# One run per partition for a scan's operand stacks, and modulation moved from the scan to a projection

## The chip, the core and the metric

The kernel runs on one core of a Trainium2 chip. The core has five engines that work beside each other and meet at semaphores: PE (matrix products), DVE (vector), ACT (scalar functions and copies), POOL (a second vector engine) and SP, which here issues almost all transfers on one queue. Sixteen DMA engines carry the packets of all queues, the packets with the engines' own instructions among them. The metric is the device time of one execution in microseconds (us); lower is better.

## The reference

Two layers act on one residual stream of 1024 latent and 256 context tokens with 1024 channels, in float32. Layer 0 mixes over time with a two-directional RWKV-7 recurrence, layer 1 with attention; each is followed by an MLP. Cut to what matters here:

```
def modulate(h, shift, scale): return h * (1 + scale) + shift

def _wkv_step(state, inp):
    r, w, k, v, kk, bvec = inp
    sa = einsum('bhvk,bhk->bhv', state, -kk)
    state = state * w[:, :, None, :] + sa[..., None] * bvec[:, :, None, :] + v[..., None] * k[:, :, None, :]
    y = einsum('bhvk,bhk->bhv', state, r)
    return state, y

for i in range(DEPTH):
    m_l = split(silu(c) @ w_mod[i] + b_mod[i], 6)         # shift, scale and gate, twice
    m_c = split(silu(c_ctx) @ w_mod[i] + b_mod[i], 6)
    h = modulate(rms_norm(x, norm_mix[i]), m[0], m[1])
    x = x + m[2] * mix(h)                                 # r, k, v projections, 2 scans, readout, wo
    x = x + m[5] * mlp(modulate(rms_norm(x, norm_mlp[i]), m[3], m[4]))
```

The scan runs over the context first, and its end states start the scans over the latent tokens.

## The kernel before

The work runs in stages: norm and first modulation parts (to about 100 us); the k projection with three small low-rank products and the modulation of layer 1 (to 345 us); the r and v projections with the preparation of the scan beside them (345 to 1025 us); the scan itself (1025 to 1523 us); readout and output projection (to 1707 us); MLP, attention, MLP.

A modulation part (`mod_part`) makes 512 of a layer's 6144 values. It loads eight tiles `wmod` of 128x512 (256 KB each), multiplies them with the activated `c` in four quarters of PE (`ps_mod`, L191), has ACT copy the sums to `mrow` (L195), and turns them with four small products (L198). Layer 0 has twelve parts. Its first four are made at the start; numbers 4 to 11 are needed only after the scan, and `mod_some` and `kick` spread them over the scan.

The scan is worked in chunks of 32 tokens: 40 steps, each for four pairs of channel tiles (`Chain.step`, pairs staggered by `staggered`). One step of one pair is four groups of eight products on PE: `ps_x` (L848) from the state `SV` and the stack, `ps_x` again (L854) with the chunk's inverse `T`, `ps_s` (L868), which gives the next state, and `ps_y` (L877), the output. Between them ACT and DVE copy results and POOL spreads the inverse (L830).

The operands of the scan lie in DRAM scratch. The tensor `d_ST` holds the stacks: for each of 128 partitions, four pairs, nine units (eight with the tiles `AR` and `G`, the ninth with the inverses `TTo`), 40 chunks, 64 values. Preparation writes it (L676 for `AR` and `G`, L720 for `TTo`). Two chunks are a granule, and every two steps `Lanes.load` fetches the next granule's parts for two of the four pairs at a time (`lp` 0 or 1): the stacks `ST` (L805), the lane states `LS` (L808, from `d_LS`), and the values `SV` (L811, from `d_V`).

Preparation (`Prep`) takes 80 half units through PE, ACT, DVE and POOL, and `weave` hands them out beside the projections. After each group of 32 chunks, `Prep.invert` inverts 32x32 triangles in 31 dependent rounds on POOL and DVE (`To` and `Tn`, L712 and L713), between two transposes on DVE (`Tm`, L699, and `TTo`, L717). There are five such inversions; the last is that of the fourth pair over the latent chunks, which the scan's first four granules, those of the context, don't need.

Each engine runs its instructions in the order in which they were written, moved by a scheduler that simulates the times when the program is built. What it thinks comes first stands first in an engine's queue and holds up what stands behind it.

Of the kernel before, what the change touches and what calls it, by code (L numbers as in the profile page):

```python
# [14 lines left out]
PSUM = bass.MemoryType.PSUM  # L15
# [3 lines left out]
KT = 8  # L19
# [7 lines left out]
NC = PB // 32  # L27
# [353 lines left out]
def rwkv_consts(k):  # L381
    k.ctile("PT", [128, KT, 2, 41], pool=k.rc)
    k.ctile("zr", [128, KT, NT // 128, 2], pool=k.rc)
    dt = lambda n, shape: k.dram.tile(shape, F32, name="d_" + n, tag="d_" + n)
    S = k.S
    S["lg1"] = dt("lg1", [128, NT])
    S["h"] = [dt(f"h{ct}", [128, NT]) for ct in range(KT)]
    S["in"] = [dt(f"in{ct}", [128, 3, NT]) for ct in range(KT)]
    S["vn"] = [dt(f"vn{ct}", [NT, 128]) for ct in range(KT)]
    S["V"] = dt("V", [2, 2, 32, 20, 2, 4, 64])  # L390
    S["LS"] = dt("LS", [2, 20, 2, 32, 4, 2, 2, 2, 64])
    S["ST"] = dt("ST", [128, 4, 9, 40, 64])


def own_rows(st, pr, u, n, half, anti):


    return st[half * 64:half * 64 + 64, pr, (half ^ anti) * 4 + u, n:n + NC].rearrange("p c e -> p (c e)")


def head_sums(k):
# [33 lines left out]
def phase_a(k, hs, ps, ls, pg):  # L435
# [3 lines left out]
    tc, nc, S = k.tc, k.nc, k.S  # L439
    hp = hs.enter_context(tc.tile_pool(name="hp", reuse_waits="tile", bufs=1, side="right"))  # L440
    h = [hp.tile([128, NT], F32, name=f"h{ct}", tag=f"h{ct}") for ct in range(KT)]
    pt = ps.enter_context(tc.tile_pool(name="pt", reuse_waits="tile", bufs=1, space=PSUM))
    with ExitStack() as e2:
        xp = e2.enter_context(tc.tile_pool(name="xp", reuse_waits="tile", bufs=1))
        wp = e2.enter_context(tc.tile_pool(name="wmp", reuse_waits="tile", bufs=8))
# [127 lines left out]
class Prep:  # L573
# [23 lines left out]
    def half(self, U, ct, blk, u0, d, B):  # L597

        k, nc, S, wk = self.k, self.k.nc, self.k.S, self.wk
        t0, n0 = blk * PB, first_chunk(d, blk)  # L600
# [72 lines left out]
        yield  # L673
        for t, anti in ((AR, 0), (G, 1)):
            for half in range(2):
                nc.sync.dma_start(out=own_rows(S["ST"], pr, ct2 * 2 + d, n0, half, anti), in_=t[half * 64:half * 64 + 64].rearrange("p c e -> p (c e)"))  # L676
        for h in range(2):
            for f in range(2):
                p = slice(h * 64 + f * 32, h * 64 + f * 32 + 32)
# [12 lines left out]
    def invert(self, Lr, dst, engs):  # L692


        k, nc, ip = self.k, self.k.nc, self.ip
        M = ip.tile([128, 2, 32, 32], F32, name="Tm", tag="Tm")
        N = [ip.tile([128, 32, 32], F32, name="Tn", tag=f"Tn{d}") for d in range(2)]
        for d in range(2):
            nc.vector.transpose(M[:, d], Lr[d].rearrange("p u j -> p j u"))  # L699
            yield  # L700
            nc.gpsimd.memset(N[d], 0.0)
            nc.gpsimd.memset(N[d].rearrange("p a b -> p (a b)")[:, 0:1024:33], 1.0)
            yield
        for i in range(31):
            for d in range(2):
                e = getattr(nc, engs[d])
                s = i if d == 0 else 31 - i
                rows, cols = (slice(s + 1, 32), slice(0, s + 1)) if d == 0 else (slice(0, s), slice(s, 32))
                r, w = rows.stop - rows.start, cols.stop - cols.start
                t = ip.tile([128, 256], F32, name="To", tag=f"To{d}")  # L710
                o = t[:, :r * w].rearrange("p (a b) -> p a b", b=w)
                e.tensor_tensor(o, M[:, d, rows, s:s + 1].to_broadcast([128, r, w]), N[d][:, s:s + 1, cols].to_broadcast([128, r, w]), ALU.mult)  # L712
                e.tensor_tensor(N[d][:, rows, cols], N[d][:, rows, cols], o, ALU.add)  # L713
                yield
        out = ip.tile([128, 32, 2, 32], F32, name="TTo", tag="Tm")
        for d in range(2):
            nc.vector.transpose(out[:, :, d].rearrange("p u j -> p j u"), N[d])  # L717
            yield
        for pr, u0, nch, n0 in dst:
            nc.sync.dma_start(out=k.S["ST"][:, pr, 8, n0:n0 + nch], in_=out[:, u0:u0 + nch].rearrange("p u d j -> p u (d j)"))  # L720
        yield

    def units(self, kinds, eng):
# [51 lines left out]
class Lanes:  # L775
# [24 lines left out]
    def load(self, k, lp, i):  # L800

        nc, S = k.nc, k.S
        ST, LS, SV = self.gp.tile([128, 2, 9, 2, 64], F32, name="ST", tag=f"ST{lp}"), self.LS[lp][i % 2], self.SV[i % 2]
        self.ST[lp, i] = ST
        nc.sync.dma_start(out=ST.rearrange("p l u c e -> p (l u) (c e)"), in_=S["ST"][:, lp * 2:lp * 2 + 2, :, 2 * i:2 * i + 2].rearrange("p l u c e -> p (l u) (c e)"))  # L805
        for h in range(2):
            anti = slice(64 - h * 64, 128 - h * 64)
            nc.sync.dma_start(out=LS[anti, h].rearrange("p l d a e c -> p (l d a e c)"), in_=S["LS"][h, i, :, :, lp * 2:lp * 2 + 2].rearrange("b s l d a f e -> (b s) (l d a f e)"))  # L808
# [197 lines left out]
def phase_ab(k, xstack):  # L1006
# [3 lines left out]
    with ExitStack() as es:  # L1010
# [13 lines left out]
        wk = ws.enter_context(tc.tile_pool(name="wk", reuse_waits="tile", bufs=1, side="right"))  # L1024
        prep, eng = Prep(k, wk, ip, pw, pg), iter(['gpsimd', 'gpsimd', 'gpsimd', 'vector', 'gpsimd', 'vector', 'gpsimd', 'vector', 'gpsimd', 'vector'])
        drain(itertools.islice(rproj, 13))
        weave(_chain([rproj, vproj]), 6 * KT - 13 + 4 + 6 * KT - LEAD, (PREP_PIECES, prep.units((0, 1, 2, None, 3), eng)))
        drain(prep.inv)
        for st in (ps, ls, ws):
            st.close()  # L1030
        mods = iter(range(5, 12))

        def mod_some(n):
            for _ in range(n):
                yield from mod_part(k, 0, next(mods), wm, pw, "pw", L)
# [15 lines left out]

        with ExitStack() as cs:
            L = Lanes(k, cs)
            wm = cs.enter_context(tc.tile_pool(name="wm", reuse_waits="tile", bufs=4))
            with tc.issue_after(k.late.ins):
                for lp in range(2):
                    L.load(k, lp, 0)
            kick = mod_part(k, 0, 4, wm, pw, "pw", L, groups=1)
            drain(itertools.islice(kick, 4))
            middle = _chain([_chain([r.center(b, False), r.scale(b, False)]) for b in (1, 2) for r in ro])  # L1060
            weave(staggered([Chain(k, L, p, y[p]).run() for p in range(4)]), 16 * Chain.n + 16, (1, kick, 12, 13), (8, kick, 16, 40), (13 * 7, mod_some(7), 16),
                  (4 * 4 + 4 * 7, early(), 16 * 5, 16 * 31), (8 * 7, middle, 16 * 33))
# [426 lines left out]
```

## Time and profile before

| | us |
|---|---|
| median of three runs | 4116.77 |
| lowest and highest run | 4102.94, 4118.79 |
| profiled execution | 4115.24 |
| its span in the trace | 4113.5 |

The profiled execution is 1.7 us longer than its span, and 1.5 us below the median. In the page, PE is busy for 3673.9 us of the span, DVE for 2179.5, POOL for 1576.1, ACT for 1523.1. PE's busy share is lowest in the preparation and in the scan, where the transfers' share is high as well; from 1605 us on PE is hardly ever idle and the transfers take a tenth to a quarter of their engines. What the change touches lies between 345 and 1523 us.

### The profile page before, as it was taken

To read this page: it belongs to the slowest core of one execution; us is meant where nothing else is said; L and a number is where in the kernel's file an instruction comes from. 1 tells how busy PE (TensorE), PEld (TensorE's weight loads), DVE (VectorE), ACT (ScalarE), POOL (GpSimd) and SP (SyncE) were. 2 spreads that over 40 slices of the span, in tenths; PEclk is the share of its full clock that TensorE was granted. 3 is DMA by queue.
4 is the path that set the end of the run, shared out by engine and by line. 5 is a ranking of instruction groups with operands and counts; after the bars stand their busy time and mean duration, and the time that the engine had idled before them with its cause. 6 is when DMAs were issued, how large, how long until landed. Compare 5 with 4: busy or idle time off the path is not lost.

```text
span 4113.5 us, 70717 instructions
## 1 busy us (share of the span) xinstructions
PE 3673.9 (89%) x28100; PEld 2803.7 (68%) x28100; DVE 2179.5 (53%) x3707; ACT 1523.1 (37%) x3222; POOL 1576.1 (38%) x1451
## 2 busy tenths in 40 slices
PE   7999866784677779999999999899999999999998
PEld 3656655673455657888888888775444477888886
DVE  6327789987653477533333333657676443333324
ACT  5656555554344443421222222433444422221122
POOL 3105686663532253521111111534787633222221
PEclk9999865885787789999999999999999999999999
DMA  8455776676888864111111111232110111111112
GB/s 286 130 161 158 176 189 160 159 185 153 211 207 202 201 164 118 60 42 36 37 36 39 39 39 44 77 101 87 32 31 16 56 42 47 46 44 49 47 53 70
DMA packets 398714, 414.77 MB, mean 101 GB/s; under 512 B 152992, under 2 KB 282272, under 8 KB 397744
## 3 DMA queue, kind: packets, MB, share of 16 engines
q1 hardware_dynamic: 397424, 408.94, 36.9%
q8 instruction: 221, 3.62, 0.4%
q0 software_dynamic: 960, 1.31, 0.2%
q14 instruction: 109, 0.89, 0.1%
HBM read 294.99 MB, written 117.11 MB: 100 GB/s over the span
## 4 chain that ended last, share of the span: by engine, by line
PE 70%; DVE 12%; issue 5%; DMA 5%; POOL 4%; ACT 2%; SPq 2%; DVEq 0%; POOLq 0%; ACTq 0%
PE ps_pj L275 47%; PE ps_av L1355 4%; PE ps_s L868 3%; PE ps_m L1232 2%; PE ps_mod L191 2%; PE ps_s L1395 2%; PE ps_s L1396 2%; POOL n_t L377 2%; PE ps_y L877 1%; PE ps_lo L419 1%; PE ps_x L848 1%; PE ps_x L854 1%; DVE To L712 1%; DVE Tn L713 1%; DMA LS<-d_LS 1%
## 5 line engine op out<-in xcount | busy, mean ns | idle before, releaser
L259 POOL TENSOR_TENSOR w_lo<-w_raw,w_hi 128x512 fp32r<-128x512 f32 (+1 forms) x292 | 475.9, 1631 | 1597.4 <-ACT w_hi L257 1549.8
L275 PE MATMUL ps_pj<-xh,w_hi 128*128 128x512 f32 (+1 forms) x1712 | 626.6, 367 | 4.2 <-ACT w_hi L257 3.8
L275 PE MATMUL ps_pj<-xh,w_lo 128*128 128x512 f32 (+1 forms) x1712 | 618.4, 365 | 8.1 <-POOL w_lo L259 8.0
L275 PE MATMUL ps_pj<-xl,w_hi 128*128 128x512 f32 (+1 forms) x1712 | 623.7, 365 | 0.6 <-DVE xl L998 0.6
L1115 DVE SCALAR_TENSOR_TENSOR xr<-ps_pj,c_mod,xr 128x512 f32<-128x512 f32 (+1 forms) x368 | 251.9, 686 | 566.6 <-PE ps_pj L275 559.8
L257 ACT CAST w_hi<-w_raw 128x512 fp32r<-128x512 f32 (+1 forms) x292 | 216.7, 742 | 836.4 <-PE ps_pj L275 645.2
L275 PE MATMUL ps_pj<-hid_l,w_hi 128*128 128x512 f32 (+1 forms) x1280 | 474.4, 371 | 0.0
L275 PE MATMUL ps_pj<-hid_h,w_hi 128*128 128x512 f32 (+1 forms) x1280 | 473.2, 371 | 0.0
L275 PE MATMUL ps_pj<-hid_h,w_lo 128*128 128x512 f32 (+1 forms) x1280 | 469.8, 370 | 0.0
L1139 DVE TENSOR_TENSOR m_q<-m_r 128x512 f32<-128x512 f32 x160 | 187.8, 1174 | 407.5 <-ACT m_r L1137 406.8
L275 PEld LDWEIGHTS ps_pj<-xh,w_lo 128*128 128x128 f32 x1712 | 323.2, 190 | 61.6 <-POOL w_lo L259 10.4
L275 PEld LDWEIGHTS ps_pj<-xh,w_hi 128*128 128x128 f32 x1712 | 325.0, 190 | 59.0 <-ACT w_hi L257 5.8
L275 PEld LDWEIGHTS ps_pj<-xl,w_hi 128*128 128x128 f32 x1712 | 324.8, 190 | 52.9 <-issue 1.4
L1406 POOL TENSOR_TENSOR acc<-acc,p 128x1024 f32<-128x1024 f32 x122 | 295.4, 2421 | 58.9 <-ACT p L1399 54.5
L275 PEld LDWEIGHTS ps_pj<-hid_h,w_hi 128*128 128x128 f32 x1280 | 241.4, 189 | 44.2
L275 PEld LDWEIGHTS ps_pj<-hid_h,w_lo 128*128 128x128 f32 x1280 | 241.1, 188 | 43.8
L275 PEld LDWEIGHTS ps_pj<-hid_l,w_hi 128*128 128x128 f32 x1280 | 241.4, 189 | 43.2
L275 PE MATMUL ps_pj<-xhi,w_hi 128*128 128x512 f32 (+1 forms) x576 | 229.4, 408 | 25.1 <-ACT xhi L479 19.6
L1399 ACT ACTIVATE p<-ps_s 128x1024 f32<-128x1024 f32 x160 | 163.8, 1024 | 230.6 <-PE ps_s L1396 229.5
L275 PE MATMUL ps_pj<-xlo,w_hi 128*128 128x512 f32 (+1 forms) x576 | 224.0, 390 | 8.8 <-DVE xlo L480 8.8
L1236 DVE TENSOR_REDUCE mc<-ps_m 128x1 f32<-128x512 f32 x256 | 174.7, 690 | 99.9 <-PE ps_m L1232 96.2
L830 POOL TENSOR_TENSOR T<-ST,c_qmask 128x256 f32<-128x256 f32 x160 | 118.9, 744 | 280.4 <-PE ps_x L854 197.0
(238 smaller groups left out, 7071.2 us busy)
## 6 DMA issues: line engine op xcount, KB each, us to landing
wmod<-in_wmod SPq DMA_DIRECT2D x192, 256.0 KB
ST<-d_ST SPq DMA_DIRECT2D x40, 1152.0 KB
w_raw<-in_m SPq DMA_DIRECT2D x64, 512.0 KB
w_raw<-in_m SPq DMA_DIRECT2D x128, 256.0 KB
d_ST<-AR SPq DMA_DIRECT2D x160, 128.0 KB
d_LS<-KT SPq DMA_DIRECT2D x320, 64.0 KB
d_ST<-G SPq DMA_DIRECT2D x160, 128.0 KB
LS<-d_LS SPq DMA_DIRECT2D x80, 256.0 KB
```

Source lines behind the costliest of these rows:

```text
L191: i = nc.tensor.matmul(ps[q:q + 32, :W], k.c["sc"][:, kt, :], w, start=(kt < groups), stop=(kt >= KT - groups), tile_position=(0, q))
L257: nc.scalar.copy(hi, raw)
L259: getattr(nc, eng).tensor_tensor(lo, raw, hi.bitcast(F32), ALU.subtract)
L275: i = nc.tensor.matmul(ps[:, :n], w[:, sl], x[:, t0:t0 + n], start=a, stop=z)
L830: k.nc.gpsimd.tensor_tensor(self.T, t.to_broadcast([128, 2, 4, 32]), k.c["qmask"].unsqueeze(1).to_broadcast([128, 2, 4, 32]), ALU.mult)
L868: nc.tensor.matmul(pst[h * 64:h * 64 + 64, ct2, d, :], ls[:, h, ln, d, ct2, :, c], sv(h, ct2, d), start=True, stop=True, tile_position=(0, ...
L1115: k.nc.vector.scalar_tensor_tensor(x[:, t0:t0 + n], ps[:, :n], g, x[:, t0:t0 + n], ALU.mult, ALU.add)
L1139: nc.vector.tensor_tensor(q[:, :n], r[:, :n], r[:, :n], ALU.mult)
L1236: line(nc.vector.tensor_reduce(mc[:, t + u, t0 // 512:t0 // 512 + 1], ps, AX.X, ALU.max), "v")
L1355: line(nc.tensor.matmul(st["av"][e * 64:e * 64 + 64], k.V[:, kt, ct // 2 * 64:ct // 2 * 64 + 64], p[:, e], start=(kt == 0), stop=(kt == 9) ...
L1399: nc.scalar.activation(p, ps, AF.Exp)
L1406: (nc.vector if ct == KT - 1 and kt % 3 == 2 else nc.gpsimd).tensor_tensor(st["acc"], st["acc"], p, ALU.add)
```

## The change

The stacks' tensor is laid out anew: `d_ST` is now ordered by partition, pair of pairs, granule, pair, unit, chunk, so that all that one load of `ST` takes lies in one piece per partition. A load that read 18 runs of 512 bytes per partition reads one of 9216 bytes. The stores pay for it: one of `AR` or `G` wrote one run of 2048 bytes per partition and now writes four of 512; one of `TTo` wrote one run of 8192 (or 2048) bytes and now writes 16 (or 4) of 512.

The modulation parts 4 to 11 of layer 0 leave the scan. `r_and_mods` hands them out beside the 35 pieces of the r projection that are left when the preparation begins, two pieces of modulation or so to one of the projection. They take their sums in the PSUM pool `pt`. The first of them, which alone was made in one piece of PE instead of four (`groups=1`), is now made like the others.

```
-    S["ST"] = dt("ST", [128, 4, 9, 40, 64])
+    S["ST"] = dt("ST", [128, 2, 20, 2, 9, 2, 64])
...
+def granules(st, pr, u, n, num, rows=slice(None)):
+    return st[rows, pr // 2, n // 2:(n + num) // 2, pr % 2, u].rearrange("p i c e -> p i (c e)")
...
-        nc.sync.dma_start(out=ST.rearrange("p l u c e -> p (l u) (c e)"), in_=S["ST"][:, lp * 2:lp * 2 + 2, :, 2 * i:2 * i + 2]...)
+        nc.sync.dma_start(out=ST.rearrange("p l u c e -> p (l u c e)"), in_=S["ST"][:, lp, i].rearrange("p l u c e -> p (l u c e)"))
...
+        rest = 6 * KT - 13
+        def r_and_mods():
+            with tc.tile_pool(name="wm", reuse_waits="tile", bufs=4) as wm:
+                weave_in = _chain([mod_part(k, 0, c, wm, k.pt, "pt") for c in range(4, 12)])
+                for n, _ in enumerate(rproj):
+                    drain(itertools.islice(weave_in, 8 * 9 * (n + 1) // rest - 8 * 9 * n // rest))
+                    yield
+                drain(weave_in)
-        weave(_chain([rproj, vproj]), 6 * KT - 13 + 4 + 6 * KT - LEAD, (PREP_PIECES, prep.units(...)))
+        weave(_chain([r_and_mods(), vproj]), rest + 4 + 6 * KT - LEAD, (PREP_PIECES, prep.units(...)))
...
-            weave(staggered([...]), 16 * Chain.n + 16, (1, kick, 12, 13), (8, kick, 16, 40), (13 * 7, mod_some(7), 16), (..., early(), ...), (..., middle, ...))
+            weave(staggered([...]), 16 * Chain.n + 16, (..., early(), ...), (..., middle, ...))
```

What this does to the queues shows at three places. The first is PE in the scan, somewhat before its middle: before, products of the modulation stand between the pairs' groups.

```order
L868 MATMUL ps_s<-SV_10461,LS_10465 64x64 x8
L877 MATMUL ps_y<-SV_10461,ST 32x64 x8
L198 MATMUL ps_mod<-c_msel,mrow 128x2
L848 MATMUL ps_x<-SV_10460,ST 32x64 x8
L854 MATMUL ps_x<-X,T 32x64 x8
L868 MATMUL ps_s<-SV_10461,LS_10465 64x64 x8
L877 MATMUL ps_y<-SV_10461,ST 32x64 x8
```

All of these `ps_mod` rows are gone from the scan. The second place is PE about the middle of what is left of the r projection, where they stand now, between projection (`ps_pj`, with the split inputs `xhi`, `xlo`) and preparation (`ps_g`, and `ps_l`, the low-rank products):

```order
L275 MATMUL ps_pj<-xlo,w_hi 128x256
L198 MATMUL ps_mod<-c_msel,mrow 128x2
L666 MATMUL ps_g<-AR,KB 64x64 x16
L198 MATMUL ps_mod<-c_msel,mrow 128x2 x3
L275 MATMUL ps_pj<-xhi,w_lo 128x256
L275 MATMUL ps_pj<-xhi,w_hi 128x256
L275 MATMUL ps_pj<-xlo,w_hi 128x256
L275 MATMUL ps_pj<-xhi,w_lo 128x256
L275 MATMUL ps_pj<-xhi,w_hi 128x256
L693 MATMUL ps_z<-c_rkb,kd 128x2 x2
```

Preparation's products stand behind them in PE's queue. The third place is SP's queue at the scan's start. Before, the store of the last inverses (`d_ST<-TTo`, 2048 values) comes after the loads of the first granules; these are the rows that end with it, the second and third granules' loads and modulation weights ahead of it:

```order
L808 DMA LS_10465<-d_LS 64x1024 x2
L811 DMA SV_10461<-d_V 32x512 x8
L186 DMA wmod<-in_wmod 128x512 x8
L808 DMA LS_10462<-d_LS 64x1024
L805 DMA ST<-d_ST 128x18x128
L808 DMA LS_10462<-d_LS 64x1024
L808 DMA LS_10464<-d_LS 64x1024
L805 DMA ST<-d_ST 128x18x128
L808 DMA LS_10464<-d_LS 64x1024
L811 DMA SV_10460<-d_V 32x512 x8
L186 DMA wmod<-in_wmod 128x512 x4
L720 DMA d_ST<-TTo 128x2048
```

Now it stands ahead of the first load of `LS` and `SV`:

```order
L560 DMA d_vn_133<-vt_sb 128x4x128
L810 DMA ST<-d_ST 128x2304 x4
L560 DMA d_vn_133<-vt_sb 128x4x128
L566 DMA d_V<-d_vn_133 32x32x64 x2
L725 DMA d_ST<-TTo 128x16x128
L813 DMA LS_10730<-d_LS 64x1024 x2
L813 DMA LS_10732<-d_LS 64x1024 x2
L816 DMA SV_10728<-d_V 32x512 x8
L813 DMA LS_10731<-d_LS 64x1024 x2
```

The four loads of `ST` (two granules, both halves) go ahead, but `LS` and `SV` of the first granule now wait in SP's queue for the last inversion. On DVE, likewise, the clearing of `SV` (L790 and L792 before) now stands behind the last inversion, where it stood between `Tm` and the rounds.

More of the change, by code (lines that the diff above doesn't have):

```diff
@@ L391, in rwkv_consts @@
     S["LS"] = dt("LS", [2, 20, 2, 32, 4, 2, 2, 2, 64])
-    S["ST"] = dt("ST", [128, 4, 9, 40, 64])
+    S["ST"] = dt("ST", [128, 2, 20, 2, 9, 2, 64])
 def own_rows(st, pr, u, n, half, anti):
-    return st[half * 64:half * 64 + 64, pr, (half ^ anti) * 4 + u, n:n + NC].rearrange("p c e -> p (c e)")
+    return granules(st, pr, (half ^ anti) * 4 + u, n, NC, slice(half * 64, half * 64 + 64))
+def granules(st, pr, u, n, num, rows=slice(None)):
+    return st[rows, pr // 2, n // 2:(n + num) // 2, pr % 2, u].rearrange("p i c e -> p i (c e)")
 def head_sums(k):
@@ L441, in phase_a @@
     h = [hp.tile([128, NT], F32, name=f"h{ct}", tag=f"h{ct}") for ct in range(KT)]
-    pt = ps.enter_context(tc.tile_pool(name="pt", reuse_waits="tile", bufs=1, space=PSUM))
+    pt = k.pt = ps.enter_context(tc.tile_pool(name="pt", reuse_waits="tile", bufs=1, space=PSUM))
     with ExitStack() as e2:
@@ L675, in half @@
             for half in range(2):
-                nc.sync.dma_start(out=own_rows(S["ST"], pr, ct2 * 2 + d, n0, half, anti), in_=t[half * 64:half * 64 + 64].rearrange("p c e -> p (c e)"))
+                nc.sync.dma_start(out=own_rows(S["ST"], pr, ct2 * 2 + d, n0, half, anti), in_=t[half * 64:half * 64 + 64].rearrange("p (i c) e -> p i (c e)", c=2))
         for h in range(2):
@@ L719, in invert @@
         for pr, u0, nch, n0 in dst:
-            nc.sync.dma_start(out=k.S["ST"][:, pr, 8, n0:n0 + nch], in_=out[:, u0:u0 + nch].rearrange("p u d j -> p u (d j)"))
+            nc.sync.dma_start(out=granules(k.S["ST"], pr, 8, n0, nch), in_=out[:, u0:u0 + nch].rearrange("p (i c) d j -> p i (c d j)", c=2))
         yield
@@ L804, in load @@
         self.ST[lp, i] = ST
-        nc.sync.dma_start(out=ST.rearrange("p l u c e -> p (l u) (c e)"), in_=S["ST"][:, lp * 2:lp * 2 + 2, :, 2 * i:2 * i + 2].rearrange("p l u c e -> p (l u) (c e)"))
+        nc.sync.dma_start(out=ST.rearrange("p l u c e -> p (l u c e)"), in_=S["ST"][:, lp, i].rearrange("p l u c e -> p (l u c e)"))
         for h in range(2):
@@ L1026, in phase_ab @@
         drain(itertools.islice(rproj, 13))
-        weave(_chain([rproj, vproj]), 6 * KT - 13 + 4 + 6 * KT - LEAD, (PREP_PIECES, prep.units((0, 1, 2, None, 3), eng)))
+        rest = 6 * KT - 13
[6 more added lines that the diff above has]
+                drain(weave_in)
+        weave(_chain([r_and_mods(), vproj]), rest + 4 + 6 * KT - LEAD, (PREP_PIECES, prep.units((0, 1, 2, None, 3), eng)))
         drain(prep.inv)
@@ L1030, in phase_ab @@
             st.close()
[L1031 to L1035, printed above, removed]
         rn = es.enter_context(tc.tile_pool(name="rn", reuse_waits="tile", bufs=1))
@@ L1053, in phase_ab @@
             L = Lanes(k, cs)
-            wm = cs.enter_context(tc.tile_pool(name="wm", reuse_waits="tile", bufs=4))
             with tc.issue_after(k.late.ins):
@@ L1057, in phase_ab @@
                     L.load(k, lp, 0)
-            kick = mod_part(k, 0, 4, wm, pw, "pw", L, groups=1)
-            drain(itertools.islice(kick, 4))
             middle = _chain([_chain([r.center(b, False), r.scale(b, False)]) for b in (1, 2) for r in ro])
-            weave(staggered([Chain(k, L, p, y[p]).run() for p in range(4)]), 16 * Chain.n + 16, (1, kick, 12, 13), (8, kick, 16, 40), (13 * 7, mod_some(7), 16),
-                  (4 * 4 + 4 * 7, early(), 16 * 5, 16 * 31), (8 * 7, middle, 16 * 33))
+            weave(staggered([Chain(k, L, p, y[p]).run() for p in range(4)]), 16 * Chain.n + 16, (4 * 4 + 4 * 7, early(), 16 * 5, 16 * 31), (8 * 7, middle, 16 * 33))
         ips.close()
```

## The prediction

> **What bounds the kernel now.** I read the chain of waits first, then windows by stage, then the scan alone.
>
> ```profile
> span 4113.5 us, 70717 instructions
> PE 70%; DVE 12%; issue 5%; DMA 5%; POOL 4%; ACT 2%; SPq 2%; DVEq 0%; POOLq 0%; ACTq 0%
> ```
>
> PE ends most steps. "Issue" is time in which PE waits for nothing that the profile shows, about 200 us. The windows, whose columns are us, busy time of PE, PEld, DVE, ACT and POOL with counts, granted clock, DMA share and GB/s:
>
> ```profile
> 345.00:450.00 105.00, 99.20 (x798) 81.96 (x797) 79.39 (x137) 65.78 (x160) 48.68 (x64) 0.97 0.72 187
> 450.00:550.00 100.00, 77.46 (x736) 65.90 (x737) 80.69 (x130) 56.06 (x148) 79.00 (x122) 0.87 0.73 173
> 650.00:750.00 100.00, 70.57 (x519) 55.18 (x517) 98.49 (x196) 58.52 (x148) 50.28 (x74) 0.61 0.72 168
> 1300.00:1400.00 100.00, 72.02 (x2137) 57.95 (x2129) 37.40 (x99) 42.96 (x168) 24.08 (x33) 0.79 0.87 204
> ```
>
> At the head of the r projection PE is full; later in the preparation DVE is. In the scan no engine is full, and the transfers fill 0.87 of their engines. The chain of waits of the scan alone (1100 to 1523 us), and its transfers:
>
> ```profile
> by line: PE ps_s L868 24.4%; issue 23.4%; PE ps_y L877 13.3%; PE ps_x L848 10.0%; PE ps_x L854 9.2%; PE ps_mod L191 4.3%; DMA LS<-d_LS 3.2%; DVE SV L872 2.5%; PE ps_mod L198 2.0%; ACT SV L861 1.2%; DMA ro_v<-d_V 0.9%; DMA SV<-d_V 0.8%; DVE
> q1 hardware_dynamic: 99435, 81.55, 81.2%
> q8 instruction: 74, 1.21, 1.3%
> ST<-d_ST SPq DMA_DIRECT2D x34, 1152.0 KB
> ```
>
> PE's products are the bound, and 23.4% of 423 us, 99 us, is "issue". Queue q8 explains it: 74 packets with 1.21 MB, 16 KB each, are PE's own instructions, one packet per 423 / 74 = 5.72 us. In the timeline the gaps lie 128 matmuls (128 weight loads beside them) apart: 256 instructions of 64 bytes are such a packet. So I cut the scan there; each window is one packet's work and the gap behind it (four in a row, which are one granule, and the scan's last, without transfers):
>
> ```profile
> 1393.04:1399.99 6.95, 3.58 (x127) 3.00 (x127) 2.44 (x7) 2.59 (x10) 1.47 (x2) 1.00 1.13 263
> 1399.99:1406.59 6.60, 5.45 (x128) 4.60 (x127) 2.52 (x8) 2.59 (x10) 1.46 (x2) 0.54 1.10 243
> 1406.59:1411.22 4.63, 4.63 (x125) 4.11 (x128) 1.21 (x4) 2.48 (x10) 1.46 (x2) 0.54 0.30 87
> 1411.22:1414.98 3.76, 3.12 (x141) 2.65 (x133) 3.04 (x8) 2.70 (x11) 1.46 (x2) 1.00 0.39 107
> 1517.64:1521.88 4.24, 3.77 (x137) 3.02 (x132) 3.84 (x11) 3.42 (x14) 0.00 (x0) 1.00 0.02 4
> ```
>
> The same 128 matmuls, give or take those in flight at a cut, take 3.8 to 4.6 us where transfers leave room, and 6.6 to 7.0 us where a load of `ST` fills the engines (share over 1.0): PE then idles for its next packet, which waits behind the load. [...]
>
> **The change part by part.**
>
> *Modulation out of the scan.* In the scan's chain L191 and L198 hold 4.3 + 2.0% of 423 us, 26.6 us: −27.
>
> *Modulation into the r projection.* PE gets those 27 us. About half falls into the first 105 us, which have no room for it (99.20 busy), half behind them, where there is room: +13. On SP and the DMA engines, 64 loads of 256 KB come to 16.8 MB (here and below, 1 MB is 10^6 bytes). The price of long rows:
>
> ```profile
> 4.00:20.00 16.00, 0.13 (x1) 0.16 (x2) 9.97 (x21) 11.05 (x23) 0.00 (x0) 1.00 0.98 375
> 1605.00:1707.00 102.00, 101.56 (x882) 93.39 (x882) 47.39 (x87) 34.89 (x71) 35.35 (x28) 0.98 0.25 76
> 1307.00:1311.00 4.00, 2.42 (x93) 2.03 (x92) 2.28 (x6) 2.04 (x9) 1.47 (x2) 1.00 1.04 235
> ```
>
> At 375 / 0.98 = 383 GB/s (input tiles) they take 44 us of full engines, at 76 / 0.25 = 304 (weights) 55. Spread over some 250 us this lifts the share from 0.72 to about 0.93: near the limit, not over it. Four buffers make SP wait for PE and PE for SP; behind a late weight stand preparation's stores on SP and its products on PE. I take +5 for that (0 to +40). ACT's eight copies fit into its idle time (65.78 of 105 busy). The mixing for v stands later, behind the last modulation weights in SP's queue; DVE's work is the same, so I add nothing.
>
> *Stores in 512-byte runs.* 320 stores of 128 KB (41.9 MB) go from 20,480 packets to 81,920, and those of `TTo` (5.2 MB) from 1024 to 10,240. No row isolates such a store. If they move like the 512-byte loads (235 / 1.04 = 226 GB/s, the last row) instead of 383, they take 185 instead of 109 us, +76 of engine time over 650 us, share +0.12. But the r stretch moves 187 GB/s at 0.72, that is 260 at full share, with most packets still shorter (43792 of 70009 under 512 bytes), so the lower end is zero. DVE covers either, unless the share reaches 1.0. I take 0 (0 to +20).
>
> ```profile
> DMA packets 70009, 52.99 MB, mean 180 GB/s; under 512 B 43792, under 2 KB 55696, under 8 KB 69850
> ```
>
> *Loads in 9216-byte runs.* One load is 1.18 MB: at 226 GB/s 5.2 us, at 383 3.1, at 304 3.9. I take 3.1, as those tiles too go to all 128 partitions in long rows. So 2.1 us less for each of 40 loads, 84 us of engine time. What of it reaches PE is the wait of one packet of instructions per load: of four windows per granule, two are caught by a load. I let these fall from 6.8 to 5.0 us, by most of the load's 2.1, as a packet may still meet `LS` or `SV`; the other two stay at 4.2, the mean of the three light rows. Mean 4.6. The scan has 40 steps of four pairs, four groups of 2560 records:
>
> ```profile
> L848 PE MATMUL ps_x<-SV,ST x2560: 216/219/316, 1044.1 to 1519.0; 128*32 128x64 f32 x197
> ```
>
> 10,240 matmuls are 80 windows: 80 x 4.6 = 368 us. At 5.72 they would be 458; the 90 us between are the 27 of modulation, about 13 of the 17 us that 3.2 + 0.8% of the chain are waits for `LS` and `SV`, and 50 of the 99 us of "issue". Ends: caught windows not shortened, 5.36 on average (5.72 less modulation's 26.6 / 74; 429 us); none caught, with the clock up, 3.8 as in the fourth row (304).
>
> *The scan's start.* It now waits for the last inversion. Before, that lay beside the first steps:
>
> ```profile
> 1016.45 1.11 PE L553 MATMUL ps_vt<-c_ident,pj_sb 128*128 128x128 f32 x4 [8.45 <-ACT vt_sb L554]
> 1044.08 3.18 PE L848 MATMUL ps_x<-SV,ST 128*32 128x64 f32 x48 [26.51 <-DMA SV<-d_V]
> 1021.51 3.73 DVE L699 STREAM_TRANSPOSE Tm<-Lr 128x1024 f32<-128x1024 f32 x2 [6.83 <-DMA d_ST<-TTo]
> 1025.15 0.61 SPq L805 DMA_DIRECT2D ST<-d_ST  x1
> 1099.85 0.37 SPq L720 DMA_DIRECT2D d_ST<-TTo  x1
> 1021.00:1093.00 72.00, 15.76 (x31) 16.24 (x31) 0.69 0.88 209
> 1021.00:1093.00 72.00, 15.36 (x31) 17.77 (x31) 0.69 0.88 209
> ```
>
> From `Tm` to the store it took 78 us, but the rounds alone (the last two rows, L712 and L713, with DVE's and POOL's busy time) need 16.24 + 17.77 = 34 us on POOL. In the new order only four spreadings of `T` come between. With transposes and gaps I put it at 47. `Tm` itself waited 6.83 us for its buffer; that store now goes out much earlier, so it starts at 1014.7 plus the 18 us of the r stretch: 1033. The store follows at 1080; behind it twelve loads are issued at about 0.55 us each (the rows below) and the last lands, 9 us, which covers the clearing of `SV` on DVE (six at 0.91): first `ps_x` at 1089. At the end, 3 us for the staggered pairs.
>
> ```profile
> 1291.97 1.09 SPq L808 DMA_DIRECT2D LS<-d_LS  x2
> 1026.67 0.91 DVE L790 MEMSET SV<- 32x1024 f32 x1 [0.25 <-issue]
> ```
>
> *Sum.* 1089 + 368 + 3 = 1460 for the end of the scan, 1523 before: −63. By terms: 18 for preparation, 27 more for the start (45 against 1044), 21 back because the old scan's first steps crept (its 479 us from 1044 to 1523 are 21 over 458), −90 for the pace, 3 for the end. From 4115.24 this gives 4052 us, and 2 more against the median, 4116.77. Nothing after 1523 us changes.
>
> **The rivals.** (1) *Slower: the inversion holds the scan.* If the r stretch saturates its queues, everything up to `Tm` slips, and SP's order leaves no cover. At 4.6 per window the gain is gone when the first `ps_x` comes at 1152, 63 us later than I put it; with a slip of 90, 4142 us. For it: the share near 0.93, SP in order, PE 0.94 busy at the head. Against it: PE has 20 to 30 us free in each later 100.
>
> (2) *The layout does nothing for PE.* Either a load's engine time stays at 5.2 us or a packet of instructions waits as long behind fewer, larger runs. Then the windows stay at 5.36, the scan takes 429 us and ends at 1521: 4113 us. [...] The same holds if the 9216-byte runs are cut up again.
>
> (3) *The gaps go altogether.* If light loads rarely meet a packet, windows average 3.8 and the clock, 0.54 behind a gap in the third row, stays up: 304 us, an end at 1396, 3988.
>
> **How the numbers follow.** Mine 0.54 (4015 to 4088: ten to fifteen us of start or 0.3 us of a window either way), rival three 0.16, rival two 0.15, rival one 0.15, of which two thirds cost over 0.5%. 0.5% (21 us) is about what a measurement can tell from no change. Faster: 0.54 + 0.16 + a little of rival one less the end of mine, 0.70; same 0.19; slower 0.11. The range of eight in ten reaches from near rival three to just over rival two: 3992 to 4116.
>
> **What would show it.** Right: the packets of q8 in the scan come 4.6 us apart, the chain's "issue" there halves, `ST` no longer fills the engines for 5 us, no `ps_mod` lies in the scan, and the first `ps_x` stands behind `TTo`. Wrong: windows still over 7 us beside `ST` (rival two); `Tm` after 1070 us (rival one); or 512-byte stores that lift the share of the preparation to 1.0.

## The result, and the profile after

The changed kernel is slower: 4140.91 us median of five runs (4134.76 to 4149.1) beside 4106.83 for the kernel before (five runs, 4102.94 to 4118.79). The ratio is 1.0076, its 95% interval 1.0052 to 1.0099. I had forecast 4052 us, 0.984. The profiled execution after took 4134.76 us with a span of 4133.0, 19.5 us more than before. It was the shortest of its five, and the profiled one before (4115.24) lay above its median, so the two profiles lie closer together than the medians. Every kernel below has one profiled execution; the times of one kernel differ by up to 21 us from execution to execution, so a difference of ten us between two scans is no more than a hint unless it comes again in other pairs.

The scan first. These rows of the view by tile give the count, the durations (ns) and the start of the first and the last product `ps_x`; the last `ps_y` ends some 4 to 5 us behind it. The first row is the kernel after; the others are two experiments told below, the layout alone (L853) and the moved modulation alone (L848). The kernel before has 1044.1 to 1519.0, as quoted in the prediction.

```profile
L853 PE MATMUL ps_x<-SV,ST x2560: 216/219/317, 1103.4 to 1535.6; 128*32 128x64 f32 x197
```
```profile
L853 PE MATMUL ps_x<-SV,ST x2560: 216/219/316, 1051.8 to 1518.4; 128*32 128x64 f32 x197
```
```profile
L848 PE MATMUL ps_x<-SV,ST x2560: 216/219/317, 1094.5 to 1538.2; 128*32 128x64 f32 x197
```

After the change the scan starts 59.3 us later (I had 45) and takes 432.2 instead of 474.9 us, 42.7 less (I had 108 less). It ends 16.6 us later; the last 3 us come behind it. So the start was a little worse than forecast, and the gain of the scan was two fifths of it. These rows cover the scan from its first to its last `ps_x`, before and after (us, busy time of PE, PEld, DVE, ACT, POOL, granted clock, share of the transfers, GB/s):

```profile
1044.10:1519.00 474.90, 351.94 (x10280) 280.54 (x10284) 242.24 (x612) 206.78 (x820) 181.56 (x239) 0.82 0.84 199
1103.40:1535.60 432.20, 309.99 (x10096) 263.92 (x10097) 222.31 (x565) 201.02 (x813) 154.96 (x193) 0.80 0.61 172
```

PE is idle for 123.0 us of the scan before and for 122.2 after. What the scan lost is busy time of PE, that of the 184 products of the modulation among it; the idle time, which the new layout was to shorten, stayed.

Four windows in a row, one granule, cut at the ends of PE's gaps as in the prediction (columns as above):

```profile
1211.53:1219.09 7.56, 3.17 (x129) 2.69 (x128) 2.76 (x8) 2.61 (x12) 1.45 (x2) 0.96 1.06 296
1219.09:1225.85 6.76, 4.38 (x127) 3.77 (x127) 2.28 (x6) 2.60 (x10) 1.45 (x2) 0.75 0.75 232
1225.85:1229.96 4.11, 4.11 (x126) 3.66 (x129) 1.44 (x4) 2.02 (x8) 1.21 (x2) 0.64 0.02 4
1229.96:1233.03 3.07, 3.07 (x136) 2.63 (x135) 2.44 (x7) 2.38 (x12) 1.59 (x3) 1.00 0.11 28
```

The two caught windows take 7.56 and 6.76 us; before they took 6.95 and 6.60, and I had put them at 5.0. Over the whole scan 79 packets of q8 come in 432 us, 5.5 us apart, where I had 4.6. The chain of waits of the scan (1100 to 1540 us) says the same: "issue" has 22.6% of 440 us, 99 us, as before (23.4% of 423).

```profile
by line: PE ps_s L873 23.1%; issue 22.6%; PE ps_y L882 13.8%; PE ps_x L853 10.2%; PE ps_x L859 9.4%; DMA ST<-d_ST 2.8%; DVE SV L877 2.7%; DVE y L967 2.1%; DVE ro_st L959 1.9%; DMA SV<-d_V 1.7%; DVE ro_st L948 1.6%; DVE ro_t L246 1.5%; DVE r
```

Now the start: SP's queue, then DVE, in the timeline after the change.

```profile
1078.11 1.25 SPq L566 DMA_DIRECT2D d_V<-d_vn  x2
1092.61 0.38 SPq L725 DMA_DIRECT2D d_ST<-TTo  x1
1093.09 4.46 SPq L813 DMA_DIRECT2D LS<-d_LS  x4
...
1103.38 2.84 PE L853 MATMUL ps_x<-SV,ST 128*32 128x64 f32 x46 [40.27 <-DMA SV<-d_V]
...
1032.15 1.95 DVE L704 STREAM_TRANSPOSE Tm<-Lr 128x1024 f32<-128x1024 f32 x1 [1.18 <-ACT Lr L676]
...
1057.69 4.87 DVE L936 COPY ro_st<-c_zr 32x10 f32<-32x10 f32 x14
1062.58 0.66 DVE L717 TENSOR_TENSOR To<-Tm,Tn 128x240 f32<-128x240 f32 x1
1063.27 3.54 DVE L936 COPY ro_st<-c_zr 32x10 f32<-32x10 f32 x14
```

`Tm` stands where I had put it (1033), but the store of `TTo` left at 1092.61 instead of 1080. Between the rounds of the last inversion DVE now makes the 64 small copies of the gates (`Readout.gates`), 20 us of DVE time. Behind that store, in SP's queue, stand all loads of `LS` and `SV`, and the scan starts 10.8 us after it. V's own last store went out at 1078.11; the same row before stood 54 us earlier:

```profile
1023.81 1.25 SPq L561 DMA_DIRECT2D d_V<-d_vn  x2
```

Some 9 of these 54 us have a cause of their own. The last products of V's projection (`ps_vt`) come 45.5 us later than before (1061.99 against 1016.45). But the store of V needs the landing of another, `d_vn<-vt_sb`, and that one now stands in SP's queue behind the first four loads of `ST`, 4.7 MB, which before came after V. SP's waits from 1060 to 1095 us show it, 11.6 us for the last one:

```profile
SPq L566 <- DMA d_vn<-vt_sb: 14.0, 2, 11.6
```

### The profile page after: what moved, and what is told of

It reads as the page before. It is cut to its first block, busy times and chain, and to the rows that moved or that the text cites. A ratio compares the mean times of both kernels' runs of the same rounds, so it can differ in the third digit from the quotient of the medians.

```text
span 4133.0 us, 70820 instructions
## 1 busy us (share of the span) xinstructions
PE 3670.7 (89%) x28100; PEld 2787.2 (67%) x28100; DVE 2194.8 (53%) x3707; ACT 1521.6 (37%) x3222; POOL 1579.6 (38%) x1451
## 3 DMA queue, kind: packets, MB, share of 16 engines
q0 software_dynamic: 960, 1.31, 0.2%
## 4 chain that ended last, share of the span: by engine, by line
PE 63%; DVE 11%; issue 5%; DMA 3%; POOL 2%; SPq 1%; ACT 1%; DVEq 0%; POOLq 0%; ACTq 0%
PE ps_pj L275 44%; PE ps_av L1360 4%; PE ps_s L873 2%; PE ps_m L1237 2%; PE ps_s L1400 2%; PE ps_s L1401 2%; POOL n_t L377 2%; PE ps_y L882 1%; PE ps_x L853 1%; DVE To L717 1%; DVE Tn L718 1%; PE ps_x L859 1%; DVE sgw L635 1%; DVE AR L652 1%; DVE KT L658 1%
## 5 line engine op out<-in xcount | busy, mean ns | idle before, releaser
L275 PE MATMUL ps_pj<-xlo,w_hi 128*128 128x512 f32 (+1 forms) x576 | 223.2, 389 | 20.6 <-DVE xlo L485 20.5
```

The source lines that it names most:

```text
L275: i = nc.tensor.matmul(ps[:, :n], w[:, sl], x[:, t0:t0 + n], start=a, stop=z)
```

## The experiments

My theory after this: the start's 59 us are the modulation's doing, through V and the copies, and PE in the scan waits for its instruction packet behind the burst of loads queued ahead of it. The rivals: the layout's short stores make the late start; the layout does nothing for the scan; the wait has another cause.

All ratios are to the kernel before on the same chip, with their 95% intervals. "Scan" in what follows is the time from the first to the last `ps_x` (474.9 before, 432.2 after); the expectations count to the end of `ps_y`, which is 4 to 5 us more. A window there is the time between two instruction packets, about 80 to a scan.

**Each part alone.** `layout` is the change without its last hunks, `mods` these alone.

```diff
 layout:
-    S["ST"] = dt("ST", [128, 4, 9, 40, 64])
+    S["ST"] = dt("ST", [128, 2, 20, 2, 9, 2, 64])
 ... (stores and load as in the change; the weave of the scan as before)
 mods:
-        weave(_chain([rproj, vproj]), ...
+        weave(_chain([r_and_mods(), vproj]), ...
 ... (kick and mod_some out of the scan; S["ST"] as before)
```

> The changed layout of the stacks alone; the modulation parts stay in the scan, where they were. Theory (the late start comes from the moved modulation parts, and the shorter ST loads give part of the scan's 42 us): first ps_x as before, at 1040 to 1052; scan 15 to 30 us shorter than 479; time 4077 to 4092 against 4107. Rival one (the stores of 512-byte pieces slow the preparation, so the layout makes the late start): first ps_x at 1065 or later, time 4105 or more. Rival two (the scan's gain comes from the modulation's loads having left it, the layout does nothing): start as before, scan 475 to 482, time 4102 to 4112.

> The moved modulation parts alone; the stacks keep their old layout and loads. Theory: V's mixing comes late and the copies of the gates stand in the last inversion, as in the changed kernel, so first ps_x at 1095 to 1105; scan 12 to 27 us shorter than 479; time 4130 to 4148 against 4107. Rival one (the layout makes the late start): first ps_x 1040 to 1055, time 4065 to 4095. Rival two (all of the scan's gain is the modulation's): start late, scan 433 to 442, time 4116 to 4124.

Measured: `layout` 0.9996 (0.9986 to 1.0006), `mods` 1.0052 (1.0038 to 1.0065). By the rows above, the layout alone starts 7.7 us later than the kernel before and then takes 8.3 us less, nothing in sum. The modulation alone starts 50.4 us later and takes 31.2 us less. Together 58.1 and 39.5, against the 59.3 and 42.7 of the change: within what single profiles can tell, the parts add up. So the slower time is the moved modulation, as the theory had it. For the scan the second rival was nearly right, since most of its gain is the modulation's products and loads that left it, and the 4077 to 4092 us that I expected of the layout did not come (4108.67).

That the layout should do so little is the surprise, because it did all that was claimed for the transfers. The queues in 1100 to 1500 us, before and with the layout alone (packets, MB, share of 16 engines):

```profile
q1 hardware_dynamic: 97657, 80.09, 84.5%
q8 instruction: 69, 1.13, 1.3%
```
```profile
q1 hardware_dynamic: 25865, 80.53, 68.5%
q8 instruction: 70, 1.15, 1.3%
```

The same bytes in a quarter of the packets, and 16 points of 400 us, 64 us, less engine time: 1.9 us for each of the 34 `ST` loads in it, against 2.1 in my sum. And q8, PE's instructions, moved by one packet in 70. With the layout alone the windows of a granule are still two long and two short:

```profile
1225.01:1232.23 7.22, 3.72 (x128) 2.71 (x128) 2.28 (x6) 2.90 (x12) 1.59 (x3) 0.92 1.00 314
1232.23:1239.71 7.48, 5.25 (x127) 4.49 (x127) 2.28 (x6) 2.60 (x10) 1.45 (x2) 0.62 1.04 304
1239.71:1243.50 3.79, 3.79 (x126) 3.34 (x127) 1.99 (x5) 1.84 (x7) 0.73 (x1) 0.70 0.44 112
```

The 7.7 us at the start go back to the short stores: ahead of the scan the layout alone changes nothing else, but for what the scheduler makes of them. V's last store leaves at 1032.88, 9.1 us later than before, and `Tm` begins at 1030.79 instead of 1021.51, both times behind a store of `TTo` that it waits for.

```profile
1030.79 3.73 DVE L704 STREAM_TRANSPOSE Tm<-Lr 128x1024 f32<-128x1024 f32 x2 [7.34 <-DMA d_ST<-TTo]
```

**The copies.** `gates` is the changed kernel with the 64 copies kept out of the last inversion: they wait for a scaling `SV<-ps_s` of the scan on DVE (`L.scaled`), not the first one, and then run from 1140 to 1251 us.

```diff
-                    self.k.nc.vector.tensor_copy(self.st[q:q + 32, 2, c::4], ...
+                    i = self.k.nc.vector.tensor_copy(self.st[q:q + 32, 2, c::4], ...
+                    self.k.order(i, L.scaled)      # L.scaled: SV<-ps_s of Chain.step
```

> The changed kernel, with the 64 copies ro_st<-c_zr on DVE kept behind the scan's first product, so that none of them stands in the last inversion. Theory (they cost the inversion their 20 us of DVE time, and V's last store at 1078 is late next): TTo's store at 1068 to 1076 instead of 1092, first ps_x at 1086 to 1093 instead of 1103, scan unchanged, time 4124 to 4132 against 4141 of the changed kernel. Rival one (something else holds the start as well, such as the loads of the first granule or T's spreading): first ps_x 1098 to 1104, time 4136 to 4145. Rival two (the copies now delay the scan's products on DVE): first ps_x early, scan 8 to 15 us longer, time 4136 to 4145.

Measured 1.0059 (1.0045 to 1.0073). The store of `TTo` left at 1083.21 instead of 1092.61, and the scan started 9.5 us earlier:

```profile
1080.16 1.25 SPq L566 DMA_DIRECT2D d_V<-d_vn  x2
1083.21 0.38 SPq L725 DMA_DIRECT2D d_ST<-TTo  x1
1083.69 4.46 SPq L813 DMA_DIRECT2D LS<-d_LS  x4
1093.94 2.95 PE L853 MATMUL ps_x<-SV,ST 128*32 128x64 f32 x48 [28.69 <-DMA SV<-d_V]
```

The mechanism holds, half its size: `Tm` came 2 us later here, and the store 7 us later than I expected. In the profiled run the scan took 445.7 us instead of 432.2, as the second rival has it, copies in the scan's DVE work. But that execution (4141.04 us) was 6 us above the median of its kernel and the one of the change 6 us below, so the rival is not shown. The interval overlaps that of the change, so what the edit brings in time is not settled.

**Without the stack's loads, and with half of them.** `nostack` loads `ST` for the first two granules only, `half` loads one pair's half of each later one. Both read older tiles for the rest, so they compute something else; all products stay.

```diff
 nostack:
+        ST = self.ST[lp, i] = ... if i < 2 else self.ST[lp, i - 2]
+        if i < 2:
           nc.sync.dma_start(out=ST..., in_=S["ST"][:, lp, i]...)
 half:
+        n = 2 if i < 2 else 1
+        nc.sync.dma_start(out=ST[:, :n]..., in_=S["ST"][:, lp, i, :n]...)
```

> The changed kernel, with ST loaded for the first two granules only; all later granules read those tiles again (36 of the 40 loads are left out, and the output is not the reference's). Theory (PE's instruction packet waits behind the loads that stand in the queues, ST's 3.8 us each among them): no window over 6 us, mean window 3.6 to 4.2 us instead of 5.4, scan 345 to 375 us instead of 437, time 4045 to 4080. Rival one (the wait is of a fixed length or has another cause, such as PE's own clock and operands): mean window 5.0 or more, scan 410 to 437, time 4110 to 4141. Rival two (the bytes matter and not the queue, the share of the DMA time falls from 0.63 to 0.3 and the waits fall with it in all windows alike): caught and light windows shrink together, scan 380 to 405.

> The changed kernel, with only the first half of each later ST load done (one pair of the two, rows of 4608 bytes; the other half is read from the tile of two granules ago, so the output is not the reference's). All 40 loads stand where they stood. Theory (the wait is the length of the burst in front of the packet): half of what leaving the loads out gave: mean window 4.8 to 5.1 (5.52 with whole loads, 4.47 with none), scan 385 to 410 (437 and 356), time 4080 to 4105. Rival one (the wait comes with each ST load, however long it is): mean 5.3 to 5.6, scan 425 to 440, time 4120 to 4141. Rival two (a short burst is free altogether): mean 4.4 to 4.7, scan 355 to 375, time 4045 to 4070.

Measured, one run each: `nostack` 4042.47 us, `half` 4083.96. Their rows of `ps_x`, `nostack` first:

```profile
L854 PE MATMUL ps_x<-SV,ST x2560: 216/219/316, 1096.3 to 1447.5; 128*32 128x64 f32 x197
```
```profile
L854 PE MATMUL ps_x<-SV,ST x2560: 216/219/316, 1100.9 to 1482.4; 128*32 128x64 f32 x197
```

The scan takes 351.2 us without loads, 381.5 with half of each, 432.2 with all: the first half of a load costs PE 30 us over the scan, the second 51. The whole scan of `nostack`:

```profile
1096.30:1447.50 351.20, 273.36 (x10094) 231.16 (x10096) 222.29 (x565) 200.01 (x813) 154.98 (x193) 0.92 0.33 90
```

Of the 81 us between none and all, 44 are idle time of PE (122.2 to 77.8) and 37 are busy time: the same products run faster, at a granted clock of 0.92 instead of 0.80. So PE does wait on these loads, by how much they load and not once for each load; `half` came out as the theory had it, `nostack` a little better. A granule of `nostack` (four windows), then two windows of `half`:

```profile
1207.53:1211.53 4.00, 3.14 (x129) 2.66 (x128) 2.33 (x7) 2.42 (x10) 1.45 (x2) 1.00 0.66 173
1211.53:1215.24 3.71, 3.17 (x128) 2.69 (x128) 2.14 (x6) 2.44 (x10) 1.46 (x2) 1.00 0.17 46
1215.24:1219.22 3.98, 3.18 (x126) 2.70 (x126) 2.42 (x7) 2.50 (x10) 1.47 (x2) 1.00 0.29 81
1219.22:1222.94 3.72, 3.11 (x128) 2.69 (x128) 2.14 (x6) 2.44 (x10) 1.46 (x2) 1.00 0.47 122
```
```profile
1230.85:1236.21 5.36, 3.11 (x128) 2.69 (x127) 2.71 (x7) 2.64 (x11) 1.46 (x2) 1.00 0.99 261
1236.21:1240.56 4.35, 4.35 (x128) 3.90 (x128) 1.44 (x4) 1.96 (x8) 1.14 (x2) 0.61 0.72 169
```

Without `ST` none of these windows is long, and even so each is 0.5 to 0.9 us longer than PE is busy in it. Their clock stays at 1.00, where with the loads the windows shown behind a gap of 2 us or more have 0.54 to 0.75.

**The loads spread.** `spread` cuts the loads of a granule in pieces, each released by the last `ps_y` that PE has been given before it, and hands them out over the eight pair-steps of the granule ahead (the place in the table is the pair-step; the numbers in an entry are the pair of pairs and the half). `lspread` does the same in `layout`, `bspread` in the kernel before, with 512-byte rows.

```diff
-            if self.pr % 2 and s % 2 == 0 and s // 2 + 1 < len(self.seq):
-                self.L.load(self.k, self.pr // 2, s // 2 + 1)
+            if s // 2 + 1 < len(self.seq):
+                self.L.load(self.k, s // 2 + 1, s % 2 * 4 + self.pr)
+    slots = ((), (("ST", 0, 0),), (("ST", 0, 1), ("LS", 0, 0)), (("LS", 0, 1), ("SV",)),
+             (("ST", 1, 0),), (("ST", 1, 1),), (("LS", 1, 0), ("LS", 1, 1)), ())
 ... (in load(), each piece of slots[j] gets a semaphore wait on self.last)
```

> The changed kernel with the loads of a granule cut in pieces (ST by halves of 0.6 MB, LS one by one) and spread over the eight pair-steps of the granule ahead, each piece released by the last ps_y product that PE has been given before it. Bytes and row lengths are the same but for ST rows of 4608 instead of 9216 bytes. Theory (PE's instruction packet waits for the burst of LS and ST that was queued as its window began, about 5.6 us; it costs the burst less some 1.6 us): with pieces of 1.9 to 2.8 us the wait is 0.5 to 1.5 us in all windows alike, no window over 6.5 us in the steady scan, mean window 4.0 to 4.7 instead of 5.5, scan 330 to 375 instead of 437 us, time 4035 to 4080. Rival one (only the sum of the loads counts, the wait is shared out anew): mean window 5.3 or more, time 4130 to 4150. Rival two (loads paced by PE come too late, PE waits for data instead of instructions): time 4110 or more, with PE waits on ST or LS loads in the list of waits.

> The same spreading in the kernel with the new layout alone (the modulation parts stay in the scan, so the start is early). Theory: first ps_x at 1044 to 1055, mean window 4.2 to 4.9 instead of 5.65, scan 350 to 405 instead of 470 us, time 4000 to 4045. Rival one (only the sum counts): 4100 to 4115. Rival two (the modulation's weight loads queue behind paced pieces and PE waits for them): scan 430 or more.

> The same spreading in the kernel before: old layout, each ST half 1152 rows of 512 bytes (2.65 us by the kernel before, against 1.9 in the new layout). Theory: pieces of 2.7 to 3.8 us cost each window 1.1 to 2.2 us: mean window 4.7 to 5.3 instead of 5.72, scan 385 to 435 instead of 479, time 4015 to 4070, and 15 to 40 us more than the same spreading with the new layout, so that here the layout pays. Rival (row length doesn't matter to the wait, as the layout alone showed no gain): within 8 us of the new layout with the same spreading.

Measured: `spread` 0.9983 (0.997 to 0.9996), `lspread` 0.9918 (0.9904 to 0.9932), `bspread` 0.9919 (0.9907 to 0.9932). Same bytes, same products: `spread` takes 404.3 us for the scan where the change takes 432.2, by this row of the view by tile.

```profile
L864 PE MATMUL ps_x<-SV,ST x2560: 216/219/317, 1091.9 to 1496.2; 128*32 128x64 f32 x197
```

So it matters how the loads stand, not only their sum; the first rival is out. But I had expected 330 to 375. One reason may be that in the built order two `ST` halves still stood side by side. And the kernel before gains as much from it as the new layout does, 4079.71 against 4080.05 us: the last rival, row length without effect, held. By the rows, `lspread` first, it scans 9.4 us faster and starts 5.7 us later.

```profile
L864 PE MATMUL ps_x<-SV,ST x2560: 216/219/317, 1044.0 to 1476.1; 128*32 128x64 f32 x197
```
```profile
L859 PE MATMUL ps_x<-SV,ST x2560: 216/219/315, 1038.3 to 1479.8; 128*32 128x64 f32 x197
```

**Spread evenly.** `even`, `leven`, `beven` are these three with another table, one `ST` half in every second pair-step. `geven` is `even` with the copies of `gates`.

```diff
+    slots = ((("ST", 0, 0),), (("LS", 0, 0), ("LS", 0, 1)), (("ST", 0, 1),), (("SV",),),
+             (("ST", 1, 0),), (("LS", 1, 0), ("LS", 1, 1)), (("ST", 1, 1),), ())
```

> The changed kernel with the spread loads placed evenly: an ST half in every second pair-step (so about one in each of PE's windows), LS pairs and SV in the pair-steps between. In the first spreading two ST halves still fell into one window, and such windows waited 2.2 to 3.5 us, while windows with one half (1.4 to 1.5 us of transfers) waited nothing. Theory (the wait is the burst that stands in the queue as the packet is asked for, less about 1.6 us that is free): mean window 4.1 to 4.6 instead of 5.1, scan 340 to 375 instead of 409, time 4045 to 4075. Rival one (cutting and pacing gain once, where a piece lands doesn't matter): mean 5.0 or more, time 4098 to 4112. Rival two (LS pairs now make the burst): windows of 4.8 to 5.5 in two of four, time 4080 to 4098.

> The same even placing in the kernel with the new layout alone, modulation parts in the scan. Theory: mean window 4.4 to 4.9 instead of 5.15 (the modulation's loads still come unpaced), scan 370 to 410 instead of 436, time 4015 to 4055. Rival (as for even): time 4073 to 4087.

> The same even placing in the kernel before, with its old layout (an ST half is 1152 rows of 512 bytes, 2.65 us). Theory one (the wait goes by the time that a burst keeps the queues busy): 0.3 to 1 us more per window than with the new layout, 15 to 50 us more in all. Theory two (the wait goes by bytes, or by what the memory gives, and the time of a short row overlaps with others'): within 8 us of the new layout with the same placing, as it was with the first spreading (4079.7 against 4080.1).

> The even placing with the copies of the gates kept out of the last inversion too. Theory: the start gains its 8 to 10 us here as well (first ps_x at 1090 to 1096), scan as in even, time 3 to 10 us under even. Rival (the copies now stand in the scan's DVE work, which a faster scan feels): time equal to even or up to 10 us more.

Measured: `even` 0.9963 (0.995 to 0.9975), `leven` 0.99 (0.9886 to 0.9913), `beven` 0.9935 (0.9923 to 0.9948), `geven` 0.9938 (0.9924 to 0.9951). All gains in the scan were smaller than expected: `even` (4091.55 us) has the time of its second rival and the pace of its first, and `leven` (4069.45) lies between its theory and its rival. Pieces still leave in bunches, as here in `even`, where from 1150 to 1400 us SP stood for 51.9 us, up to 5.9 at a time, until a `ps_y` released an `ST` piece; how much of the shortfall this makes was not tested:

```profile
1202.68 0.36 SPq L817 DMA_DIRECT2D ST<-d_ST  x1
1203.14 1.81 SPq L821 DMA_DIRECT2D LS<-d_LS  x2
1205.04 4.02 SPq L817 DMA_DIRECT2D ST<-d_ST  x2
```

Between `leven` and `beven` row length counts for the first time: 4069.45 against 4082.03 us, intervals apart. Their rows, `leven` first:

```profile
L864 PE MATMUL ps_x<-SV,ST x2560: 216/219/316, 1043.3 to 1471.7; 128*32 128x64 f32 x197
```
```profile
L859 PE MATMUL ps_x<-SV,ST x2560: 216/219/316, 1037.7 to 1486.6; 128*32 128x64 f32 x197
```

The new layout starts 5.6 us later and scans 20.5 us faster. The 12.6 us between the two times lie a little under the low end of theory one.

`geven` (4086.21 us, 5 under `even`, as expected, though the intervals just touch) starts at 1083.9, the earliest of the kernels with the modulation moved. There the loads of `LS` and `SV` stand ahead of the store of `TTo`, and the loads wait for V's store alone:

```profile
1076.49 1.25 SPq L566 DMA_DIRECT2D d_V<-d_vn  x2
1077.84 1.36 SPq L821 DMA_DIRECT2D LS<-d_LS  x2
1079.30 3.95 SPq L827 DMA_DIRECT2D SV<-d_V  x8
1088.84 0.39 SPq L725 DMA_DIRECT2D d_ST<-TTo  x1
```

Yet the next products there wait for DVE's clearing of `SV`, which stands behind the rounds of the inversion and ends only 1 us later:

```profile
1085.07 1.93 PE L864 MATMUL ps_x<-SV,ST 128*32 128x64 f32 x42 [0.34 <-DVE SV L797]
```

That splits the 59 us roughly: some 40 are left when copies and the store of `TTo` are out of the way (1083.9 against 1044.1), and there V's lateness and the inversion on DVE end together, so that neither alone would give them back. Some 10 are the copies (`gates`), and some 10 the store of `TTo` ahead of the loads (1093.9 against 1083.9), in which V's store is 3.7 us earlier too.

**Finer pieces.** `lfine` is `leven` with the `LS` loads one by one in the odd pair-steps.

```diff
+    slots = ((("ST", 0, 0),), (("LS", 0, 0),), (("ST", 0, 1),), (("LS", 0, 1), ("SV",)),
+             (("ST", 1, 0),), (("LS", 1, 0),), (("ST", 1, 1),), (("LS", 1, 1),))
```

> The new layout alone with the even placing, and the LS loads taken singly: one ST half in each even pair-step, one LS load in each odd one. Theory: no window has more than about 3 us of transfers ahead of its packet; mean window 4.7 to 5.0 instead of 5.11, scan 400 to 420 instead of 432, time 4050 to 4066 against 4069. Rival (PE's release of the pieces and the modulation's loads, which come unpaced, bunch them again): time 4064 to 4078.

Measured 0.9926 (0.9908 to 0.9944), 4082.24 us: no gain, if anything a loss against `leven`, and above even the rival's 4064 to 4078. `leven` is the best version here and beats both kernels: 4069.45 us, 1% under the kernel before. It keeps the layout and leaves the modulation in the scan.

## Why the prediction was wrong

*Preparation, +18.* Right at the place that I named, by luck: `Tm` at 1032 to 1035 against 1033. I gave the stores in 512-byte runs nothing; alone they cost 9.3 us there (1021.51 to 1030.79). I counted the modulation's 18 us from 1014.7, where `Tm` would have started without the wait for its buffer; the modulation alone, which has no such wait, moved it to 1024.70, by 10:

```profile
1024.70 1.90 DVE L699 STREAM_TRANSPOSE Tm<-Lr 128x1024 f32<-128x1024 f32 x1 [3.43 <-ACT Lr L671]
```

*Start, 27 more.* Mis-sized; the start came at 1103.4 instead of 1089. Two steps failed here. "DVE's work is the same, so I add nothing" was said of the mixing for v: V's last store went out 54 us later, 9 of them behind the loads of `ST` that I had seen go ahead and not priced, and with V's store alone ahead of the loads the scan started at about 1084 (`geven`). And between `Tm` and the store I counted rounds, transposes and spreadings, 47 us; it took 60, as the scheduler had put 20 us of copies there (49.5 without them, in `gates`). As both parts were late by nearly the same time, removing one gained only 10.

*Modulation out of the scan, 27 us.* Right: `mods` alone shortens the scan by 31.2 us.

*Pace, the rest of the 90, and the old crawl, 21.* This step failed. Their sum with the scan's end is 108, of which 42.7 came, and 31 of those are the modulation's. The load did become shorter by what I said, 1.9 us for 2.1. The step that failed is the next one: "I let these fall from 6.8 to 5.0 us, by most of the load's 2.1". They stayed at 6.8 to 7.6, and PE's idle time over the scan at 122 us. The sign that I had named for it, a window over 7 us beside `ST`, came as well. Rival two, "a packet of instructions waits as long behind fewer, larger runs", describes the result; its 429 us for the scan against 437 (1103.4 to the last `ps_y`). It got 0.15, and its time, 4113, was still too low, since the start was 14 us late on top.

What the runs put in its place: PE's packet does wait behind the `ST` loads (81 us of the scan with the clock that the waits cost), by how much they load, and less if they stand apart (28 us by spreading alone). Engine time saved by longer rows was worth far less. In pairs that differ in the layout alone, the scan gained 8.3, 11.5 (`mods` to the change), 9.4 (`bspread` to `lspread`) and 20.5 us, and its start lost 7.7, 8.9, 5.7 and 5.6. Each is little more than the scatter of single profiles, but the sign is the same four times. Halving the bytes gained 51. So the 64 us of engine time that the layout frees were mostly not what the packet waited for.

Why engine time and wait come apart so far is in part open. The traces show that the gaps are the packet's: PE has 42 gaps over 0.8 us in the scan before and 43 with the layout alone, and in both the middle eight tenths of them end 2.5 to 3.0 us after a packet of q8 has begun. They also show that the new layout lets SP put more ahead of that packet. With short rows, SP was held up in issuing the `LS` load behind a load of `ST`; with long rows it hardly was. Before, then with the layout alone:

```profile
1252.70 0.53 SPq L805 DMA_DIRECT2D ST<-d_ST  x1
1253.28 7.71 SPq L808 DMA_DIRECT2D LS<-d_LS  x1
```
```profile
1250.82 0.53 SPq L810 DMA_DIRECT2D ST<-d_ST  x1
1251.40 1.44 SPq L813 DMA_DIRECT2D LS<-d_LS  x1
```

The 68 issues of `LS` from 1100 to 1500 us take 179 us of SP before and 36 with the layout. I take PE to ask for its next packet when it goes on with the one at hand (2.7 us after that one has begun, the median), which no trace shows, and look at the packets that begin more than 2 us later. At that moment the bytes issued and not yet begun were 1.14 MB before and 1.45 MB with the layout, and the packet began 4.1 and 4.4 us later, by when 1.09 and 1.31 MB had begun (medians). So it went when about as many bytes had gone as stood ahead of it: the loads ran faster, but more of them stood there. That this is the whole reason is not shown, as no run held SP's issuing equal.

The clock has a part as well. A gap of 2.25 us of idle PE (`half`, 5.36 less 3.11) is followed by a window at clock 0.61, in which PE is busy for 4.35 us instead of 3.11. By these numbers, an estimate of mine, a gap that only shrinks to some 2.5 us keeps its price behind it.

*The range, 3992 to 4116.* It ended at rival two with the start on time. The case that came was rival two with a late start, two failures that I had priced one at a time; what lay above it was left to rival one.

## What to carry to other kernels

Less engine time is a gain for PE only if PE waited for engine time, and here 64 us less of it came with a scan 8 us shorter; before pricing such a saving in full, leave the load out once and halve it once, and see which of bytes, packets and place PE follows. Where instruction packets share the DMA engines with bulk loads, as here, spread the loads over the work that they feed: here that gave 1%, and the kernel before needed no new layout for most of it. A step that is moved moves others through the scheduler: read in the new order what now stands between the rounds of every dependent chain, what stands in SP's queue behind each late store, and which late store now stands behind a burst of loads.

## What the runs showed that I had not expected

- Without `ST` loads PE's clock is granted at 1.00 in all windows of the granule shown; with them, the windows shown behind a gap of 2 us or more run at 0.54 to 0.75, and the same 128 matmuls then take 3.8 to 5.5 us of PE instead of 3.1 to 3.2.
- Even in `nostack`, where nothing but `LS` and `SV` is loaded, the windows shown are 3.7 to 4.0 us long for 3.1 to 3.2 us of products: in these windows 128 matmuls of 64 columns do not quite cover the arrival of the next packet of instructions.
- The same 80 MB in a quarter of the packets took 19% less engine time (84.5 to 68.5% of 400 us), and the scan was 8 us of 475 shorter.
